# Hybrid diffusion trunk on one core: one head order in the recurrence, 128-row rate projections, and both ends of the last expert stage reordered

## The chip, the core and the metric

The kernel runs on one core of a Trainium2 chip, as one program with five engines: TensorE (PE) multiplies matrices and writes to PSUM, VectorE (DVE) and ScalarE (ACT) do elementwise work and empty PSUM, GpSimd (POOL) does elementwise work in SBUF, and SyncE (SP) issues most of the DMAs. Each engine works through its own list in order. The metric is the device time of one execution in microseconds (us).

## The reference, cut to what matters

Two layers of one trunk over 512 latent tokens and a prefix of 256 context tokens, width 1024, fp32. Each layer has a mixer and a routed mixture of experts:

```python
# mixer, one of three branches: RWKV-7, 8 heads of 64, in two directions d
a = sigmoid(a0 + al @ a_up);  decay = exp(-exp(-softplus(-(w0 + tanh(wl) @ w_up)) - 0.5))
sa = S @ kk                                  # per token, S is 64 x 64 per head
S = S * decay - outer(sa, kk * a) + outer(v, kd);   y = S @ r
# experts: 16, each takes the top 64 latent tokens (and 32 context tokens, layer 1 only)
hid = silu(xin @ w1) * (xin @ w3);  out[idx] += (hid @ w2) * gate
```

`w_up` and `a_up` are 64 x 512 for each direction. An expert has three matrices of 1024 x 1024 fp32, 12 MB. Only the latent tokens are returned, so the second layer emits no context tokens: its recurrence still runs through the context to get the state, without `y`.

## The kernel before

**Recurrence (`rwkv_phase`, L890).** Heads are worked in four pairs, the two heads of a pair in partitions 0 to 63 and 64 to 127 of the projected tiles, and the 768 tokens in 12 chunks of 64. Both directions go together (index d). So a layer has 48 chunks, each with a *window* (`window`, L636), which needs no state, and a *chain* (`chain`, L760), which carries the state from chunk to chunk. A window scales keys and queries by the decays (`kc`, `kr`), multiplies them on PE into a PSUM slot, masks the products into `sc` and `sv` (L700, L701), and inverts a triangular 64 x 64 system per head by six levels of doubling in fp16 (`nb`, `wt`, `xt`, `xx`; `xtr` is the inverse). A chain multiplies state and values with `sv` (`pz`), solves with `xtr`, corrects once, and makes the next state (`V`, L844) and `y`. Windows run up to three chunks ahead.

In this kernel the row order differs for the two heads: for head h the score rows of `kk` lie in half h and those of `k` in the other half, so each mask or scaling is done once for each head on 64 partitions:

```python
for h in range(2):
    hs, ho = slice(64 * h, 64 * h + 64), slice(64 - 64 * h, 128 - 64 * h)
    v.tensor_tensor(g.sc[hs, :, :nm, hs], ps[hs, :, h, :nm], self.scc[hs, :, :nm], ALU.mult)
    v.tensor_tensor(g.sv[ho, :, :nm, h], ps[ho, :, h, :nm], self.scc[ho, :, :nm], ALU.mult)
```

The state half of `V` and the value half change places with h in the same way; `rows` (L546) and `value_rows` (L751) lay the values out to match.

**Rates (`rates`, L554).** For each pair, segment and direction two matmuls multiply the low-rank activations `wal` (rows 0 to 63 for the decay, 64 to 127 for the learning rate) with `ups`, each on its own 64 rows: 64 matmuls in the two layers.

**Fill.** The input projections that the recurrence does not need soon (`unit`, L142: `pw` tiles with their `w_hi` and `w_lo` parts) and, in the first layer, parts of the modulation (`piece`, `pa`) are handed out behind the chain, 6.0 us of PE time a chunk in the first layer and 3.0 us in the second (`self.fills`, L1874); what is left when the last chain is done runs at the end of the phase (`self.spend(1e9)`). The order on each engine is laid down before the run by a planner, which simulates a timeline with costs of its own and takes the instruction of highest priority that its timeline has ready.

**Experts of the second layer (`experts`, L1513).** `pick` (L1583) builds the one-hot matrices `gl` of four experts, then the gates (`pga`, `gcol`) and transposed one-hots (`pgt`, `gt`); `gather` (L1641) multiplies the tokens (`xhi`, `xlo`) with `gl` into `pxi` and evicts them to `xin`, for each of eight slices of the width. `hidden` (L1690) then takes `w1` and `w3` in pairs of 1 MB (`load_e`, L1668). Twelve loads of 1 MB have buffers; the first twelve are issued ahead, and each later one waits on SP until PE has read the buffer that it overwrites. `output` (L1730) multiplies with `w2`; after each second expert `scatter` (L1783) weighs the result with gate and modulation, splits it in `yhi` and `ylo`, multiplies by `gt` (`psc`) and adds to the residual `xr` (L1803), and the end of the kernel stores `xr` from SP (L1578).

Of the kernel before, what the change touches and what calls it, by code (L numbers as in the profile page):

```python
# [19 lines left out]
P = 128  # L20
D = 1024
KT = 8
# [45 lines left out]
class Trunk:  # L68
# [168 lines left out]
    def consts(self, ctx):  # L237
# [6 lines left out]
        self.id64 = cp.tile([P, 64], F32, name="id64")  # L244
        nc.vector.tensor_tensor(self.id64, self.ident[:, 0:64], self.ident[:, 64:128], ALU.add)
# [235 lines left out]
    def lora(self, full):  # L481
# [3 lines left out]
        self.ups = rp.tile([P, 2, P], F32, name="ups")  # L485
# [12 lines left out]
    def pair(self, p, full):  # L498
# [7 lines left out]
        def load():  # L506
            for d in range(2):
                cs = slice(p * P, (p + 1) * P)
                nc.sync.dma_start(self.ups[0:64, d], self.i["rwkv_w_up"][self.l, d, :, cs])
                nc.sync.dma_start(self.ups[64:128, d], self.i["rwkv_a_up"][self.l, d, :, cs])  # L510
# [36 lines left out]
        def rows(s):  # L547

            self.need(q.u["value"])
            b0, nb = SEGB[s]  # L550
            vt = q.vt[s] = rp.tile([P, 2 * nb, HD], F32, name="vt", tag=f"vt{s}")
            self.requarter(q.v[:, b0 * P:], nb, lambda c, h: vt[64 - 64 * h:128 - 64 * h, c::2])

        def rates(s):  # L554
# [5 lines left out]
            if s == 0:  # L560
                q.f = rp.tile([P, 2, NCH], F32, name="f", tag="f", bufs=2)
                q.lm = rp.tile([P, 2, NCH], F32, name="lm", tag="lm")
            nc.gpsimd.memset(D[:, 0, :, 0:1], 0.0)
            nc.gpsimd.memset(D[:, 1, :, 64:65], 0.0)
            for d in range(2):
                w0, a0 = self.w0h[:, 4 * d + p:4 * d + p + 1], self.a0h[:, 4 * d + p:4 * d + p + 1]
                ps = self.bank()
                self.mm(ps[:, :n], self.ups[0:64, d], self.wal[0:64, a:a + n], True, True)
# [11 lines left out]
                self.mm(ps[:, :n], self.ups[64:128, d], self.wal[64:128, a:a + n], True, True)  # L580
# [14 lines left out]
            nc.scalar.activation(q.f[:, :, x], q.f[:, :, x], AF.Exp, scale=S_DEC)  # L595

# [39 lines left out]
    def window(self, q, n, emit, kb):  # L636
# [43 lines left out]
        g.sv = rp.tile([P, 2, 2, 2, 64], F32, name="sv", tag="sv", bufs=4)  # L680
        for h in range(2):
            hs, ho = slice(64 * h, 64 * h + 64), slice(64 - 64 * h, 128 - 64 * h)
            v.tensor_tensor(kc[hs, :, ho], two(q.k)[hs], t1[hs], ALU.mult)
            v.tensor_tensor(kc[hs, :, hs], kk[hs], t2[hs], ALU.mult)
            dst = g.sv[hs, :, :nm, h]
            if n:
                f = q.f[hs, :, n - 1, None, None].to_broadcast([64, 2, nm, 64])
                pl.tensor_tensor(dst, kr[hs, :, h, :nm], f, ALU.mult)
            else:
                pl.tensor_copy(dst, kr[hs, :, h, :nm])  # L690
        yield

        bank = self.slots[n % 3]
        ps = bank.rearrange("p (d h m i) -> p d h m i", d=2, h=2, m=2)
# [19 lines left out]
        nb = mat("nb")  # L714
        nc.gpsimd.tensor_tensor(
            nb, g.sc[:, :, 0], self.ident[:, None].to_broadcast([P, 2, P]), ALU.add
        )
        x = xt = None
        for l in range(6):
# [24 lines left out]
            else:  # L744
                xt = mat("xtr", F32R, "xtr", 4)
# [5 lines left out]
    def value_rows(self, q, n):  # L751

        t = self.rp.tile([P, 2, 2, HD], F32, name="V", tag="V", bufs=3)
        s, z0, z1, _ = seg_chunks(n)
        for h in range(2):
            ho = slice(64 - 64 * h, 128 - 64 * h)
            self.nc.gpsimd.tensor_copy(t[ho, :, h], self.two(q.vt[s][ho], z0, z1))
        return t

    def chain(self, q, n, V, emit):  # L760
# [4 lines left out]
        halves = [slice(0, 64), slice(64, 128)]  # L765
        if n == 0:
            V = self.value_rows(q, 0)
            for h, hs in enumerate(halves):
                nc.gpsimd.memset(V[hs, :, h], 0.0)
        last = n == NCH - 1  # L770
        out = None if last else self.value_rows(q, n + 1)
        if n and not last:
            sf = rp.tile([P, 2, HD], F32, name="sf", tag="sf")
            fc = q.f[:, :, n - 1]
            for h, hs in enumerate(halves):
# [22 lines left out]
        sa = first = None  # L798
# [39 lines left out]
        if emit:  # L838
# [1099 lines left out]
```

## Time and profile before

| | |
|---|---|
| Median of 3 runs | 3648.34 us (3643.23 to 3650.91) |
| Profiled execution, device time | 3643.64 us |
| Its span (first to last instruction) | 3641.9 us |
| PE busy | 3367.1 us (92%) |
| DVE busy | 1950.3 us (54%) |
| ACT busy | 1289.5 us (35%) |
| POOL busy | 1133.7 us (31%) |
| Weights of the experts (`we`) | 384 DMAs of 1 MB |

A busy PE is not PE at its peak: a matmul's recorded time holds its latency, and the next one starts before it ends. So PE's pace is read from start to start. An fp32 matmul has two records, an fp32r matmul one. A granted clock of 1.00 is 2.4 GHz, 0.50 is 1.2 GHz. Idle time of an engine that is not the bottleneck costs nothing; what matters is what PE or, in the second layer's expert stage, the DMA engines wait for.

### The profile page before, as it was taken

To read this page: it belongs to the slowest core of one execution; us is meant where nothing else is said; L and a number is where in the kernel's file an instruction comes from. 1 tells how busy PE (TensorE), PEld (TensorE's weight loads), DVE (VectorE), ACT (ScalarE), POOL (GpSimd) and SP (SyncE) were. 2 spreads that over 40 slices of the span, in tenths; PEclk is the share of its full clock that TensorE was granted. 3 is DMA by queue.
4 is the path that set the end of the run, shared out by engine and by line. 5 is a ranking of instruction groups with operands and counts; after the bars stand their busy time and mean duration, and the time that the engine had idled before them with its cause. 6 is when DMAs were issued, how large, how long until landed. Compare 5 with 4: busy or idle time off the path is not lost.

```text
span 3641.9 us, 56218 instructions
## 1 busy us (share of the span) xinstructions
PE 3367.1 (92%) x20863; PEld 2243.8 (62%) x20863; DVE 1950.3 (54%) x4725; ACT 1289.5 (35%) x3233; POOL 1133.7 (31%) x1729
## 2 busy tenths in 40 slices
PE   6999999999998989999999898888899989799998
PEld 3777777777987882233333477676678968543342
DVE  6687878764665461121222577878864665412122
ACT  3354555543454211111111345555553542211111
POOL 3555465543320410000000255656554303100000
PEclk9999999999998989999999899999999989899999
DMA  5323132334106336778888410111113154499998
GB/s 182 101 67 98 35 110 67 123 120 144 47 33 222 121 123 253 288 294 327 328 319 335 153 57 29 36 37 39 36 51 101 36 177 157 186 409 409 409 409 350
DMA packets 297045, 620.94 MB, mean 171 GB/s; under 512 B 19258, under 2 KB 160532, under 8 KB 296772
## 3 DMA queue, kind: packets, MB, share of 16 engines
q1 hardware_dynamic: 293028, 605.30, 46.0%
q0 software_dynamic: 1728, 6.29, 0.5%
q10 hardware_dynamic: 2016, 5.77, 0.4%
q8 instruction: 165, 2.70, 0.3%
q14 instruction: 108, 0.88, 0.1%
HBM read 584.00 MB, written 33.29 MB: 170 GB/s over the span
## 4 chain that ended last, share of the span: by engine, by line
PE 50%; DVE 9%; DMA 2%; ACT 2%; issue 2%; POOL 1%; DVEq 0%; ACTq 0%; POOLq 0%
PE ph L81 13%; PE pw L81 6%; PE py L81 6%; PE pc L81 4%; PE po L81 3%; PE slot L81 2%; PE pt L81 2%; PE psc L81 2%; PE pyc L81 2%; PE ba L81 2%; PE pz L85 2%; DMA we<-in_exp_w 2%; PE py L85 1%; PE pxi L81 1%; DVE wt L725 1%
## 5 line engine op out<-in xcount | busy, mean ns | idle before, releaser
L81 PE MATMUL ph<-we,xin 128*64 128x512 f32 x2048 | 513.3, 605 | 5.4 <-DVE hid L1721 2.8
L81 PE MATMUL pw<-hhi,w_hi 128*128 128x512 f32 (+1 forms) x1272 | 490.7, 390 | 15.0 <-ACT w_hi L132 6.7
L81 PE MATMUL pw<-hlo,w_hi 128*128 128x512 f32 (+1 forms) x1272 | 451.2, 359 | 0.0
L81 PE MATMUL pw<-hhi,w_lo 128*128 128x512 f32 (+1 forms) x1272 | 450.9, 360 | 0.3 <-POOL w_lo L134 0.3
L134 POOL TENSOR_TENSOR w_lo<-w_raw,w_hi 128x1024 fp32r<-128x1024 f32 x124 | 300.5, 2429 | 357.2 <-ACT w_hi L132 296.8
L81 PEld LDWEIGHTS ph<-we,xin 128*64 128x64 f32 x2048 | 151.0, 139 | 325.8 <-issue 315.2
L1793 POOL TENSOR_TENSOR ylo<-y,yhi 128x512 fp32r<-128x512 f32 x28 | 35.2, 1281 | 889.3 <-ACT yhi L1792 889.3
L725 DVE TENSOR_TENSOR wt<-slot,lvm 128x256 f16<-128x256 f32 x576 | 230.3, 418 | 94.0 <-PE slot L81 66.1
L81 PEld LDWEIGHTS pw<-hhi,w_hi 128*128 128x128 f32 x1272 | 243.6, 193 | 45.0 <-ACT w_hi L132 8.0
L81 PEld LDWEIGHTS pw<-hhi,w_lo 128*128 128x128 f32 x1272 | 242.1, 192 | 36.1 <-issue 2.6
L81 PEld LDWEIGHTS pw<-hlo,w_hi 128*128 128x128 f32 x1272 | 244.5, 193 | 30.6 <-issue 12.3
L132 ACT ACTIVATE w_hi<-w_raw 128x1024 fp32r<-128x1024 f32 x168 | 177.0, 1057 | 239.7 <-DMA w_raw<-in_w_in 77.8
L81 PE MATMUL py<-we,hT 128*64 128x512 f32 x1024 | 249.3, 607 | 8.3 <-DMA we<-in_exp_w 3.0
L742 ACT ACTIVATE xx<-slot 128x256 f16<-128x256 f32 x384 | 145.9, 382 | 162.8 <-PE slot L81 137.5
L1720 ACT ACTIVATE sl<-ph 64x512 f32<-64x512 f32 x64 | 37.8, 591 | 449.4 <-PE ph L81 429.7
L1803 DVE TENSOR_TENSOR xr<-xr,psc 128x512 f32<-128x512 f32 x144 | 90.4, 681 | 195.5 <-PE psc L81 195.4
L1721 DVE TENSOR_TENSOR hid<-sl,ph 64x512 f32<-64x512 f32 x64 | 44.1, 690 | 268.3 <-ACT sl L1720 267.9
L81 PEld LDWEIGHTS py<-we,hT 128*64 128x64 f32 x1024 | 70.3, 138 | 153.0 <-issue 134.4
L81 PE MATMUL pt<-w_hi,hhi 128*128 128x256 f32 x544 | 155.8, 288 | 5.4 <-ACT xk L1117 2.0
L81 PE MATMUL pt<-w_lo,hhi 128*128 128x256 f32 x544 | 155.5, 286 | 3.4 <-POOL w_lo L134 3.4
L81 PE MATMUL pt<-w_hi,hlo 128*128 128x256 f32 x544 | 154.7, 285 | 0.0
L81 PE MATMUL slot<-xt,wt 128*128 128x128 f16 x960 | 132.2, 224 | 21.6 <-DVE wt L725 21.1
(412 smaller groups left out, 7661.9 us busy)
## 6 DMA issues: line engine op xcount, KB each, us to landing
we<-in_exp_w SPq DMA_DIRECT2D x384, 1024.0 KB
w_raw<-in_w_in SPq DMA_DIRECT2D x124, 512.0 KB
ada_w<-in_ada_w SPq DMA_DIRECT2D x96, 512.0 KB
w_raw<-in_w_branch SPq DMA_DIRECT2D x24, 512.0 KB
w_raw<-in_w_out SPq DMA_DIRECT2D x20, 512.0 KB
gd<-gt SPq DMA_DIRECT2D x24, 384.0 KB
g<-gd SPq DMA_DIRECT2D x24, 384.0 KB
gd<-gt SPq DMA_DIRECT2D x24, 256.0 KB
```

The lines of the kernel that those rows point to most:

```text
L81: return self.leg(self.nc.tensor.matmul(out, lhsT, rhs, start=start, stop=stop))
L85: return self.leg(self.nc.tensor.matmul(out, lhsT, rhs, start=start, stop=True, skip_group_check=True))
L132: nc.scalar.activation(hi, raw, AF.Copy)
L134: self.lo_eng.tensor_tensor(lo, raw, hi.bitcast(F32), ALU.subtract)
L725: v.tensor_tensor(wt, ps, self.lvm[:, :, l], ALU.mult)
L742: nc.scalar.activation(x, ps2, AF.Copy)
L1720: nc.scalar.activation(sl, ph[0:64, ns], AF.Silu)
L1721: v.tensor_tensor(hid[0:64, ns], sl, ph[64:128, ns], ALU.mult)
L1793: (v if by_block else self.ylo_eng[nh]).tensor_tensor(lo, yn, hi.bitcast(F32), ALU.subtract)
L1803: v.tensor_tensor(x, x, pt, ALU.add)
```

## The change

Both heads now use one row order: `kk` rows in partitions 0 to 63, `k` and value rows in 64 to 127, and the head is an index of the free dimension. The scalings of `kc` and the masks are one instruction for both heads; the value half of `sv` is a POOL copy of `sc`; `nb` becomes two POOL instructions into a persistent, zeroed block-diagonal tile; the first solution `x1` is evicted by two ACT instructions, one for each head, and the second solution goes to PE straight from `V`, without its own copy. The rate projections get 128 rows with zeros in the unused half. In the second layer's expert stage the gather of the first group runs two slices at a time between the weight loads of its first expert, its gates come after that expert's `hidden`, and the last expert's `w2` is loaded by halves of its columns, each half scattered and stored from SP and ACT when it is done.

```diff
-        self.ups = rp.tile([P, 2, P], F32, name="ups")
...
+        self.ups = rp.tile([P, 2, 2, P], F32, name="ups")
+        nc.gpsimd.memset(self.ups, 0.0)
...
-            vt = q.vt[s] = rp.tile([P, 2 * nb, HD], F32, name="vt", tag=f"vt{s}")
-            self.requarter(q.v[:, b0 * P:], nb, lambda c, h: vt[64 - 64 * h:128 - 64 * h, c::2])
+            vt = q.vt[s] = rp.tile([P, nb, 2, HD], F32, name="vt", tag=f"vt{s}")
+            pt = self.bank().rearrange("p (b t) -> p b t", t=P)
+            for b in range(nb):
+                self.tr(pt[:, b], q.v[:, (b0 + b) * P:(b0 + b + 1) * P])
+            nc.scalar.activation(vt.rearrange("p b h x -> p b (h x)"), pt[:, :nb], AF.Copy)
...
+                q.fs = rp.tile([P, 2, 2, NCH], F32, name="f", tag="f", bufs=2)
+                q.f = q.fs[:, 0]
...
-                self.mm(ps[:, :n], self.ups[0:64, d], self.wal[0:64, a:a + n], True, True)
+                self.mm(ps[:, :n], self.ups[:, 0, d], self.wal[:, a:a + n], True, True)
...
-                self.mm(ps[:, :n], self.ups[64:128, d], self.wal[64:128, a:a + n], True, True)
+                self.mm(ps[:, :n], self.ups[:, 1, d], self.wal[:, a:a + n], True, True)
...
+            nc.gpsimd.tensor_copy(q.fs[0:64, 1, :, x], q.f[64:128, :, x])
...
-
-        kc, kr, g.sc = kb
+        kc, kr, g.sv, nb = kb
...
-            pl.tensor_tensor(kr[hs, :, h, 0], kk[hs], at(e, False)[hs], ALU.mult)
+            pl.tensor_tensor(kr[hs, :, 0, h], kk[hs], at(e, False)[hs], ALU.mult)
             if emit:
-                pl.tensor_tensor(kr[hs, :, h, 1], two(q.r)[hs], at(e, True)[hs], ALU.mult)
+                pl.tensor_tensor(kr[hs, :, 1, h], two(q.r)[hs], at(e, True)[hs], ALU.mult)
...
-        g.sv = rp.tile([P, 2, 2, 2, 64], F32, name="sv", tag="sv", bufs=4)
+        v.tensor_tensor(kc[:, :, 64:128], two(q.k), t1, ALU.mult)
+        v.tensor_tensor(kc[:, :, 0:64], kk, t2, ALU.mult)
         for h in range(2):
-            hs, ho = slice(64 * h, 64 * h + 64), slice(64 - 64 * h, 128 - 64 * h)
-            v.tensor_tensor(kc[hs, :, ho], two(q.k)[hs], t1[hs], ALU.mult)
-            v.tensor_tensor(kc[hs, :, hs], kk[hs], t2[hs], ALU.mult)
-            dst = g.sv[hs, :, :nm, h]
+            hs = slice(64 * h, 64 * h + 64)
...
+        g.sc = rp.tile([P, 2, 2, 2, 64], F32, name="sc", tag="sc", bufs=4)
...
-            self.mm(ps[:, d, :, :nm], kc[:, d], kr[:, d, :, :nm], True, True)
-        for h in range(2):
-            hs, ho = slice(64 * h, 64 * h + 64), slice(64 - 64 * h, 128 - 64 * h)
-            v.tensor_tensor(g.sc[hs, :, :nm, hs], ps[hs, :, h, :nm], self.scc[hs, :, :nm], ALU.mult)
-            v.tensor_tensor(g.sv[ho, :, :nm, h], ps[ho, :, h, :nm], self.scc[ho, :, :nm], ALU.mult)
+            self.mm(ps[:, d, :nm], kc[:, d], kr[:, d, :nm], True, True)
+        if emit:
+            fl = lambda t: t.rearrange("p d m h i -> p (d m) h i")
+            mask = self.scc.rearrange("p d m i -> p (d m) i")[:, :, None].to_broadcast([P, 4, 2, 64])
+            v.tensor_tensor(fl(g.sc), fl(ps), mask, ALU.mult)
+        else:
+            mask = self.scc[:, :, 0, None].to_broadcast([P, 2, 2, 64])
+            v.tensor_tensor(g.sc[:, :, 0], ps[:, :, 0], mask, ALU.mult)
+        pl.tensor_copy(g.sv[64:128, :, 0], g.sc[64:128, :, 0])
...
-        nb = mat("nb")
-        nc.gpsimd.tensor_tensor(
-            nb, g.sc[:, :, 0], self.ident[:, None].to_broadcast([P, 2, P]), ALU.add
-        )
+        for h in range(2):
+            hs = slice(64 * h, 64 * h + 64)
+            pl.tensor_tensor(
+                nb[hs, :, hs], g.sc[0:64, :, 0, h], self.ident[0:64, None, 0:64].to_broadcast([64, 2, 64]), ALU.add
+            )
...
-        s, z0, z1, _ = seg_chunks(n)
-        for h in range(2):
-            ho = slice(64 - 64 * h, 128 - 64 * h)
-            self.nc.gpsimd.tensor_copy(t[ho, :, h], self.two(q.vt[s][ho], z0, z1))
+        s, *z, _ = seg_chunks(n)
+        for d in range(2):
+            c = 64 * (z[d] % 2)
+            self.nc.gpsimd.tensor_copy(t[64:128, d], q.vt[s][c:c + 64, z[d] // 2])
...
-            sf = rp.tile([P, 2, HD], F32, name="sf", tag="sf")
-            fc = q.f[:, :, n - 1]
-            for h, hs in enumerate(halves):
-                nc.gpsimd.tensor_tensor(
-                    sf[hs], V[hs, :, h], fc[hs, :, None].to_broadcast([64, 2, HD]), ALU.mult
-                )
-
-
-        own = list(enumerate(halves))
-        both = lambda t, d: t[:, d, None].to_broadcast([P, 2, HD])
+            sf = rp.tile([64, 2, 2, HD], F32, name="sf", tag="sf")
+            f = q.fs[lo, :, :, n - 1].rearrange("p h d -> p d h")[:, :, :, None].to_broadcast([64, 2, 2, HD])
+            nc.gpsimd.tensor_tensor(sf, V[lo], f, ALU.mult)
...
-                    v.tensor_tensor(r[hs], zz[hs, :, h], sa[hs], ALU.subtract)
+                    v.tensor_tensor(r[hs], zz[hs, :, h], x1[lo, :, h], ALU.subtract)
...
-                sa = rp.tile([P, 2, HD], F32, name="sa", tag="sa", bufs=2)
-                nc.scalar.activation(sa, aa, AF.Copy)
+                for h, hs in own:
+                    nc.scalar.activation(x1[lo, :, h], aa[hs], AF.Copy)
                 self.mark()
                 for d in range(2):
-                    self.mma(zz[:, d], g.sc[:, d, 0], both(sa, d))
+                    self.mma(zz[:, d], g.sc[:, d, 0], x1[:, d])
...
-                nc.scalar.activation(V[hs, :, h], aa[hs], AF.Copy)
+                nc.scalar.activation(V[lo, :, h], aa[hs], AF.Copy)
             else:
-                v.tensor_copy(V[hs, :, h], aa[hs])
-        if emit:
-            sa = rp.tile([P, 2, HD], F32, name="sa", tag="sa", bufs=2)
-            nc.scalar.activation(sa, aa, AF.Copy)
+                v.tensor_copy(V[lo, :, h], aa[hs])
...
-                self.mma(yy[:, d], g.sc[:, d, 1], both(sa, d))
+                self.mma(yy[:, d], g.sc[:, d, 1], V[:, d])
...
-                    v.tensor_tensor(out[hs, :, h], pss[hs, :, h], sf[hs], ALU.add)
+                    v.tensor_tensor(out[lo, :, h], pss[hs, :, h], sf[:, :, h], ALU.add)
...
                 g = self.pick(0, full, post, aff)
-                self.gather(g, full, xhi, xlo)
+                ahead = self.gather(g, full, xhi, xlo)
+                if full:
+                    ahead = [None for _ in ahead] and None
+                else:
+                    next(ahead)
+            if not full:
+
+                hid0 = self.hidden(0, full, g, ahead)
+                self.group_gates(g, 0, full, aff)
             due, prev = [], None
...
                 due = []
-                if e:
+                if e == NE and not full:
+                    self.last_output(e - 1, *prev, g2r)
+                elif e:
                     due = self.output(e - 1, full, *prev, g2r)
                 if e % 4 == 3 and e < NE - 1:
                     with tc.high_priority(self.gather_hp):
                         nxt = new if full else self.pick(e // 4 + 1, full, post, aff)
-                        self.gather(nxt, full, xhi, xlo)
+                        if not full:
+                            self.group_gates(nxt, e // 4 + 1, full, aff)
+                        for _ in self.gather(nxt, full, xhi, xlo):
+                            pass
                 prev = hid, g
                 g = nxt or g
             with tc.high_priority(self.norm_hp):
                 for args in sorted(due, key=lambda t: t[-2]):
...
+            if k % 2:
+                yield
...
             ws = load(c)
+            if ahead and c:
+                next(ahead, None)
...
+    def last_output(self, ge, hid, g, g2r):
 
         nc, ep, psg = self.nc, self.ep, self.psg
...
         for nh in range(2):
+            ns = slice(nh * 512, nh * 512 + 512)
+            py = self.psy.tile([P, 512], F32, name="py", tag=("py", "py1")[nh])
+            for c in range(2):
+                pool = self.xwp[self.n_we % len(self.xwp)]
+                self.n_we += 1
+                w = pool.tile([P, 4, 512], F32, name="we", tag="we")
+                nc.sync.dma_start(
+                    w, self.i["exp_w2"][self.l, ge, c * 512:(c + 1) * 512, ns].rearrange("(k p) n -> p k n", p=P)
+                )
+                for kk in range(4):
+                    k = 4 * c + kk
+                    r = 64 * (k % 2)
+                    self.mm(py[r:r + 64], hT[:, k], w[:, kk], k < 2, k > 5)
+            odd = ep.tile([64, 512], F32, name="odd", tag="s", bufs=2)
+            nc.scalar.copy(odd, py[64:128])
+            v.tensor_tensor(self.y[64:128, ns], odd, py[0:64], ALU.add)
+            with self.tc.high_priority(self.norm_hp):
+                self.scatter(self.y, g.gcol[:, 1:2], g2r[0], g.gt[:, 1], 2, 4, by_block=True, halves=(nh,))
+                for b in range(2, NB):
+                    (nc.sync, nc.scalar)[b % 2].dma_start(self.out[0, (b - 2) * P:(b - 1) * P, ns], self.xs[b][:, ns])
```

## Rows read from the trace of the kernel before

**Rows 1.** Windows: stretch, length; busy us (instructions) PE, PEld, DVE, ACT, POOL; clock, DMA, GB/s.
```profile
110.00:870.00 760.00, 722.87 (x5231) 575.49 (x5229) 559.95 (x1458) 375.31 (x1098) 389.99 (x694) 0.99 0.29 95
2110.00:2750.00 640.00, 575.44 (x3958) 443.54 (x3957) 489.12 (x1308) 341.09 (x1002) 371.31 (x670) 0.97 0.13 41
2750.00:2786.00 36.00, 33.79 (x149) 26.74 (x148) 10.58 (x22) 11.77 (x21) 16.14 (x7) 1.00 0.42 137
3150.00:3160.00 10.00, 10.00 (x60) 6.26 (x62) 0.91 (x3) 3.65 (x7) 0.00 (x0) 1.00 0.29 97
3160.00:3170.00 10.00, 10.00 (x40) 2.88 (x38) 0.52 (x2) 2.48 (x3) 0.00 (x0) 1.00 0.76 265
3170.00:3620.00 450.00, 427.75 (x1958) 170.07 (x1954) 88.34 (x153) 57.98 (x107) 17.64 (x14) 0.97 1.03 409
3620.00:3630.00 10.00, 7.35 (x32) 2.03 (x32) 1.77 (x3) 1.03 (x3) 0.00 (x0) 1.00 0.37 147
```

**Rows 2.** PE's waits in 110 to 870: waiter <- releaser, us, times, longest.
```profile
PE pz L85 <- DVE V L844: 8.5, 18, 0.9
...
PE pw L81 <- DVE pv L456: 0.3, 1, 0.3
```

**Rows 3.** PE's waits in 2110 to 2770.
```profile
PE slot L81 <- DVE wt L725: 16.1, 23, 2.4
...
PE slot L108 <- DVE sv L701: 9.4, 18, 1.1
...
PE bk L81 <- DVE bv L612: 1.4, 2, 0.7
PE pz L85 <- ACT sa L827: 0.8, 2, 0.4
```

**Rows 4.** PE's timeline at a 64-row rate matmul: start, us, what.
```profile
2141.08 0.40 PE L81 MATMUL pw<-hlo,w_hi 128*128 128x512 f32 x1
2141.40 1.12 PE L81 MATMUL bk<-wal,ups 64*128 64x512 f32 x2
2142.46 0.73 PE L81 MATMUL pw<-hhi,w_lo 128*128 128x512 f32 x2
```

**Rows 5.** PE's timeline at a 128-row fp32 matmul of 512 columns.
```profile
157.32 1.02 PE L81 MATMUL bk<-bv,bones 128*128 128x512 f32 x2
158.18 0.28 PE L81 MATMUL slot<-xx,nb 128*128 128x128 f16 x2
```

**Rows 6.** Groups by form, whole span: out<-in, shape, count | busy us, mean ns | idle before.
```profile
L688 POOL TENSOR_TENSOR sv<-kr,f 64x256 f32<-64x256 f32 x152 | 100.6, 662 | 26.2 <-PE py L85 19.2 <-PE pz L85 0.2
L1803 DVE TENSOR_TENSOR xr<-xr,psc 128x512 f32<-128x512 f32 x144 | 90.4, 681 | 195.5 <-PE psc L81 195.4
L684 DVE TENSOR_TENSOR kc<-kk,t 64x128 f32<-64x128 f32 x192 | 78.6, 409 | 5.9 <-POOL t L666 5.4
L715 POOL TENSOR_TENSOR nb<-sc,ident 128x256 f16<-128x256 f32 x96 | 76.0, 792 | 50.6 <-DVE sc L700 48.8
L701 DVE TENSOR_TENSOR sv<-slot,scc 64x256 f32<-64x256 f32 x160 | 67.4, 421 | 3.3
L813 ACT ACTIVATE sa<-pz 128x128 f32<-128x128 f32 x96 | 27.3, 284 | 25.2 <-PE pz L85 24.7 <-DVE wt L725 0.3
```

**Rows 7.** Timeline of all engines, start of the second layer's expert stage.
```profile
3139.88 0.61 PE L85 MATMUL pga<-aff,gl 128*128 128x17 f32 x2 [0.78 <-DVE gl L1591]
...
3145.17 2.56 DVE L1540 TENSOR_TENSOR xlo<-xn,xhi 128x1024 fp32r<-128x1024 f32 x2
3145.28 0.55 PE L81 MATMUL pxi<-gl,xhi 128*128 128x256 f32 x1 [0.34 <-DVE gcol L1625]
...
3156.08 0.37 SPq L1675 DMA_DIRECT2D we<-in_exp_w  x1
```

**Rows 8.** Timeline at the end of the kernel.
```profile
3626.21 1.94 PE L81 MATMUL py<-we,hT 128*64 128x512 f32 x8 [0.59 <-DMA we<-in_exp_w]
...
3634.01 3.32 SPq L1578 DMA_DIRECT2D out<-xr  x4
```

More of the change, by code (lines that the diff above doesn't have):

```diff
@@ L764, in chain @@
         g = q.win.pop(n)
-        halves = [slice(0, 64), slice(64, 128)]
+        lo = slice(0, 64)
         if n == 0:
             V = self.value_rows(q, 0)
-            for h, hs in enumerate(halves):
-                nc.gpsimd.memset(V[hs, :, h], 0.0)
+            nc.gpsimd.memset(V[lo], 0.0)
         last = n == NCH - 1
@@ L797, in chain @@
         begin(zz, lambda d: g.sv[:, d, 0])
-        sa = first = None
+        x1 = self.x1[n % 2]
+        first = None
         for it in range(2):
@@ L897, in rwkv_phase @@
             self.psz = st.enter_context(tc.tile_pool(reuse_waits="tile", name="psz", bufs=1, space=PSUM))
-            kc, kr, sc = (
-                [self.rp.tile(shape, F32, name=f"{n}{a}") for a in range(m)]
-                for n, m, shape in (("kc", 2, [P, 2, P]), ("kr", 2, [P, 2, 2, 2, 64]), ("sc", 4, [P, 2, 2, P]))
+            kc, kr, sv, nb, self.x1 = (
+                [self.rp.tile(shape, dt, name=f"{n}{a}") for a in range(m)]
+                for n, m, shape, dt in (
+                    ("kc", 2, [P, 2, P], F32), ("kr", 2, [P, 2, 2, 2, 64], F32), ("sv", 4, [P, 2, 2, 2, 64], F32),
+                    ("nb", 3, [P, 2, P], F16), ("x1", 2, [P, 2, 2, HD], F32))
             )
-            for t in kr + sc:
+            for t in kr + sv + nb + self.x1:
                 nc.gpsimd.memset(t, 0.0)
@@ L949, in ahead @@
                         if n + a not in gens:
-                            gens[n + a] = self.window(q, c, full or c >= 4, (kc[c % 2], kr[c % 2], sc[(n + a) % 4]))
+                            gens[n + a] = self.window(q, c, full or c >= 4, (kc[c % 2], kr[c % 2], sv[(n + a) % 4], nb[c % 3]))
                         do(lambda: next(gens[n + a], None))
@@ L1557, in experts @@
                 if e < NE:
-                    hid = self.hidden(e, full, g)
+                    hid = hid0 if e == 0 and not full else self.hidden(e, full, g)
                 if full and e % 4 == 2 and e < NE - 2:
@@ L1575, in experts @@
                     self.scatter(*args, by_block=True)
-            if not full:
-                for b in blocks:
-                    nc.sync.dma_start(self.out[0, (b - 2) * P:(b - 1) * P, :], self.xs[b])
     def pick(self, grp, full, post, aff):
@@ L1602, in pick, with group_gates @@
                 )
+        if full:
+            self.group_gates(g, grp, full, aff)
+        return g
+    def group_gates(self, g, grp, full, aff):
+        nc, ep, psg = self.nc, self.ep, self.psg
+        v = nc.vector
+        gl, gc = g.gl, g.gc
         pt = psg.tile([P, 3, NE + 1], F32, name="pga", tag="g")
@@ L1680, in by_turns @@
     @staticmethod
-    def by_turns(latents, context, full, load):
+    def by_turns(latents, context, full, load, ahead=None):
         for c in range(4):
             ws = load(c)
+            if ahead and c:
+                next(ahead, None)
             fs = (latents, context) if full else (latents,)
@@ L1688, in by_turns, with hidden @@
                 f(c, *ws)
-    def hidden(self, ge, full, g):
+    def hidden(self, ge, full, g, ahead=None):
         nc, ep = self.nc, self.ep
@@ L1781, in output, with scatter @@
         return due
-    def scatter(self, y, gcol, g2r, gt, b0, nb, by_block=False):
+    def last_output(self, ge, hid, g, g2r):
         nc, ep, psg = self.nc, self.ep, self.psg
         v = nc.vector
-        hl = []
-        for nh in range(2):
+        hT = ep.tile([P, KT, CL], F32, name="hT", tag="hT")
+        for j in range(2):
+            pt = psg.tile([P, 4, CL], F32, name="phd", tag="g")
+            for q in range(4):
+                k = 4 * j + q
+                nc.tensor.transpose(pt[:, q], hid[:CL, k * P:(k + 1) * P], self.ident[:CL, :CL])
+            (nc.scalar.copy if j else v.tensor_copy)(hT[:, 4 * j:4 * j + 4], pt)
+        for nh in range(2):
+            ns = slice(nh * 512, nh * 512 + 512)
[18 more added lines that the diff above has]
+                    (nc.sync, nc.scalar)[b % 2].dma_start(self.out[0, (b - 2) * P:(b - 1) * P, ns], self.xs[b][:, ns])
+    def scatter(self, y, gcol, g2r, gt, b0, nb, by_block=False, halves=(0, 1)):
+        nc, ep, psg = self.nc, self.ep, self.psg
+        v = nc.vector
+        hl = {}
+        for nh in halves:
             yn = y[:, nh * 512:nh * 512 + 512]
@@ L1793, in scatter @@
             (v if by_block else self.ylo_eng[nh]).tensor_tensor(lo, yn, hi.bitcast(F32), ALU.subtract)
-            hl.append((hi, lo))
-        order = [(nh, b) for nh in range(2) for b in range(nb)]
+            hl[nh] = hi, lo
+        order = [(nh, b) for nh in halves for b in range(nb)]
         for nh, b in sorted(order, key=lambda t: t[1]) if by_block else order:
```

28 lines of the change are left out of this document (13 added, 15 removed).

## The prediction

> **What bounds the kernel now.** I read the busy shares by engine first, then the stretches, then what PE waits for in each stretch, and last the timelines at the places that the change touches. PE is the busiest engine in both recurrences, the DMA engines in the second layer's expert stage.
>
> In both recurrence stretches PE shows 95% and 90% busy, and DVE comes next with 560 of 760 us (74%) and 489 of 640 us (76%) [rows 1]. Behind the last chain runs what is left of the fill: from 2750 to 2786 PE is 94% busy with DVE at 29% [rows 1], and the code lays out the first layer's end in the same way. So each recurrence ends when PE has done its whole list, not when the chain is done, and a recurrence takes PE's own time plus PE's stalls. The stalls that end with a DVE instruction are 23.8 us in the first layer (eight rows, the longest 8.5 us for the next state, the shortest 0.3 us) [rows 2] and 53.0 us in the second (eight rows, from 16.1 us for `wt` to 1.4 us) [rows 3].
>
> The expert stage of the second layer differs. From 3170 us on the DMA engines move 409 GB/s without a gap, until about 3623.6 us (share 0.37 of the slice from 3620, against 1.03) [rows 1]. Its length is set by when the weight stream starts and what follows its last load. The thirteenth load is issued at 3156.08 us [rows 7].
>
> Layer 1's expert stage, both attentions and merges keep their work; I cost them at nothing.
>
> **The change part by part.**
>
> *Rate projections, 128 rows.* The fp32r matmul before the 64-row one keeps PE for 0.23 us (the pace of its neighbours, 0.23 to 0.24 us from start to start), so PE is free at 2141.31; the 64-row matmul starts at 2141.40, the next at 2142.46: 1.15 us [rows 4]. A 128-row fp32 matmul of 512 columns takes 158.18 - 157.32 = 0.86 us [rows 5]. The streaming time is the same; the difference of 0.29 us stands at the change of tile shape and back. With 64 such matmuls: 64 x 0.29 = 18.6 us of PE time. Those of 256 columns I take to save the same, since the loss is at the two ends. PE's list sets the end, so this is on the path; I take 17 us, and 0 to 18.6 for the range, as a saved gap can become a wait for data. The other way round, the skill speaks against padding: the Trainium skill, TensorEngine Tiling (Array Packing), Performance Considerations, says of a contraction of 64 that it should be tiled by rows, for up to twice the throughput. By that rule the decay and learning-rate matmuls, in opposite halves of the rows, would share 0.86 us and the padding would lose time. Here they stand alone between full-height matmuls, as in the row, and the trace does not agree.
>
> *DVE in the windows.* In an emitting window four `kc` instructions of about 0.409 us become two; an instruction's time follows its elements for each partition (128 here, before and after), so this saves 0.82 us. Four mask instructions of 0.421 us become one of 512 elements for each partition out of PSUM, for which I take the 0.681 us of the residual addition: 1.00 us less [rows 6]. Of 96 windows 80 emit, 16 save about 1.5 us: 80 x 1.82 + 16 x 1.5 = 170 us of DVE, 85 us in each layer, and DVE falls from about 75% to about 63% of the stretch. That is no time by itself. It buys back part of PE's stalls. The 9.4 us in which the `kc` transposes wait for the last mask [rows 3] should mostly go, since one mask of 0.68 us stands there in place of four of 1.68 us together: 8 us. Of the other 67 us (23.8 + 53.0 - 9.4) I take a quarter, 16 us: these are waits inside the chain and the doubling, where the DVE instruction itself stays and only the queue before it shortens. So 24 us. The ends are 0 (the list is laid out ahead, and PE may meet the next late instruction at once) and 77 us (all DVE stalls). What is late next is ACT, at 53% of the second layer's stretch [rows 1].
>
> *Longer hops.* `x1` is two ACT instructions in series, each near the 0.284 us of the one that it replaces [rows 6]: up to 96 x 0.28 = 27 us of chain latency. Queued behind them on ACT are the evictions of the doubling (`xx`, `xt`); PE waits for both. In emitting chunks the second `sa` copy goes, so ACT's sum stays; PE now waits for `V` there, which it needs anyway. PE's wait for `sa` is 0.8 us in the whole second stretch [rows 3], because fill lies between: I take 2 us, range -1 to 27. On POOL the value half of `sv` is one more copy of 64x256, at most 0.66 us by the multiplication of that shape, and `nb` is two halves for one of 0.79 us [rows 6]; `sf` is one instruction for two. POOL is at 51% and 58% [rows 1]. The copy lies between mask and chain, a chunk ahead of its use: 2 us, range 0 to 30. What waits in POOL's queue behind it is `nb`, and DVE's `xt` behind that. The extra zeroings at the head of each recurrence are hidden by the fill that runs there; without that cover they cost about 1 us a layer. The value layout (`rows`) loses two DVE copies a segment, and `id64` one instruction at the start, both in DVE's slack of a quarter of the stretch.
>
> *Start of the last expert stage.* Gates and one-hot transposes hold PE from 3139.88 us, and the first `pxi` comes at 3145.28 [rows 7]. With the gates behind `hidden` it can start at about 3140, limited by `xlo` of the last two blocks, which DVE does at 3145.17 after the gate columns [rows 7] and can now do right after `gl`, at about 3141 to 3143.5. Now 10.8 us lie between the first `pxi` and the thirteenth load (3156.08 - 3145.28), since PE takes several slices of `pxi` ahead of the first weights. With two slices ahead it should not take longer, so from 3140 the load comes at 3150.8 or earlier; the wait for `xlo` eats what the fewer slices save. No other DMA waits in front of it on SP. The stream of 180 loads takes 180 x 1.0486 MB / 409 GB/s = 461.5 us, against 3623.6 - 3156.1 = 467.5 us now; the slices of 29% and 76% [rows 1] show the starving. So the gain is 5.3 us of start and up to 6 us of starving; I take 7, range 0 (the planner leaves the gates in front) to 11. The gates, about 4 us of PE, move to where DMA covers them; if PE were the bound there, they would cost these 4 us.
>
> *End.* After the last load PE works 1.94 us from 3626.21, then come the evictions, weighting, splitting, eight additions and four stores, the first issued at 3634.01 [rows 8]; the span ends at 3641.9. After the change four additions remain behind the last load, 4 x 0.68 = 2.7 us less, one more step (the sum of the two halves, 0.68) is added, and the first half's additions can stand in DVE's queue before it, about 1 us. Stores are of half the size, on two queues. I take 1.5 us, range -4 to +3: four loads with rows of 2 KB have no row here, and I take them at the stream's pace.
>
> **Sum.** -17 - 24 + 2 + 2 - 7 - 1.5 = -45.5 us against the profiled execution's 3643.64, or 3598. That execution lies 4.7 us under the median of 3648.34; on the median's scale it is 3603 us, which I forecast.
>
> **The rivals.**
>
> *DVE was not what PE waited for.* The stalls are placed by the planner's order, and PE meets an equal stall elsewhere. Then only the matmul shape and both ends count: -17 + 4 - 8.5 = -21.5, or 3627 us. For it: PE's waits are spread over many releasers of a few us each [rows 2, 3]. Against: nearly all of them are DVE's.
>
> *DVE was the pace of both recurrences.* Most of 77 us goes, and the stream starves less: -18 - 65 + 2 - 11 = -92, or 3556 us. For it: 75% busy in an ordered queue. Against: PE is at 95% in layer 1, and its stalls there are 24 us.
>
> *POOL's new copy is late (slower).* The value half of `sv` now goes DVE, POOL, PE. POOL also carries the `w_lo` subtractions and works in order. If a copy is late by one such place in the queue, the first matmul of a chunk waits; at 0.8 us, about the `nb` ahead of it [rows 6], for all 96 chunks that is 77 us, less the 45.5: +31, or 3680 us. It decides when the copy's lead over its chunk falls under the queue in front of it. For it: `nb`, 0.79 us, waits 48.8 us for the masks already. Against: windows run a chunk ahead, some 13 us (640 us for 48 chunks).
>
> *It does not do what it says.* The planner lays out everything anew, and gains and new stalls cancel: 3648 us, within 7.
>
> **How the numbers follow.** Forecast (3588 to 3615) 0.42; only shape and ends (3615 to 3641) 0.24; DVE's pace (below 3588) 0.16; cancelled (within 0.2%, 3641 to 3656) 0.08; POOL late (above 3656) 0.10. 0.2%, some 7 us, is about what a measurement can tell from no change. Faster is 0.42 + 0.24 + 0.16 = 0.82, same 0.08, slower 0.10. The range leaves about 0.1 on each side: 3566 to 3645 us.
>
> **What would show it.** Right: the rate matmuls at 0.86 us from start to start; DVE's busy time 150 us or more lower; PE's waits for `V`, `wt` and the masks under 60 us together; the thirteenth load near 3150 minus what the recurrences gave; 409 GB/s from there. Wrong: PE's waits for POOL's `sv` or ACT's `x1` above 10 us; gates before the first `pxi`; a recurrence as long as now with DVE at 63%. The prediction falls if the two recurrences together give back less than 15 us.

## The result and the profile after

The changed kernel takes 3592.65 us (median of 4 runs, 3586.59 to 3597.45), the kernel before, on the same chip, 3647.66 us (3643.23 to 3650.91). The ratio is 0.9856, with a 95% interval of 0.9845 to 0.9868: 55 us or 1.4% faster, 10 us below the forecast of 3603 and inside the forecast's own range of 3588 to 3615. The profiled execution took 3593.62 us, its span 3591.8.

The busy shares of the changed kernel: busy us, share of the span, instructions.

```profile
PE 3332.6 (93%) x20863; PEld 2243.1 (62%) x20863; DVE 1799.7 (50%) x4213; ACT 1293.5 (36%) x3234; POOL 1193.1 (33%) x1861
```

DVE lost 150.6 us, POOL gained 59.4, ACT stayed. The stretches that answer to [rows 1], columns as there:

```profile
110.00:858.00 748.00, 715.35 (x5267) 579.87 (x5265) 484.75 (x1214) 377.33 (x1094) 422.51 (x765) 0.98 0.30 96
2100.00:2702.00 602.00, 552.90 (x3939) 440.00 (x3938) 417.46 (x1047) 343.17 (x1009) 400.22 (x730) 0.97 0.14 44
2702.00:2745.00 43.00, 40.30 (x200) 33.01 (x199) 11.29 (x24) 14.54 (x23) 20.42 (x11) 1.00 0.42 132
3130.00:3560.00 430.00, 412.25 (x1897) 163.50 (x1895) 84.79 (x147) 56.01 (x103) 17.64 (x14) 0.98 1.02 406
```

In the second layer's recurrence DVE is down from 76% to 69% and PE up from 90% to 92%; the last stage still moves weights at 406 GB/s. PE's waits of the changed kernel, 110 to 858 and then 2100 to 2760 (waiter <- releaser: us, times, longest), answer to [rows 2, 3]:

```profile
PE slot L81 <- DVE wt L735: 8.2, 8, 2.6
PE pz L85 <- DVE zr L809: 3.8, 5, 2.2
...
PE pz L85 <- DVE V L850: 0.8, 1, 0.8
```

```profile
PE slot L81 <- DVE wt L735: 22.3, 17, 4.7
PE pz L85 <- DVE zr L811: 4.4, 7, 1.9
PE slot L81 <- ACT xt L756: 4.2, 10, 0.8
...
PE slot L108 <- DVE sc L706: 3.3, 2, 2.5
```

The wait for the last mask fell from 9.4 us to 3.3, that for the next state nearly vanished, and the wait for `wt` grew from 16.1 to 22.3. All rows that end with DVE together fell from 23.8 to 14.5 us and from 53.0 to 36.4. No row names POOL's copy of `sv`.

The groups of the new instructions (busy us, mean ns), beside [rows 6]:

```profile
L706 DVE TENSOR_TENSOR sc<-slot,scc 128x512 f32<-128x512 f32 x80 | 55.3, 691 | 10.5 <-PE slot L81 8.2 <-PE py L85 0.5
L819 ACT ACTIVATE x<-pz 64x128 f32<-64x128 f32 x192 | 51.6, 269 | 25.6 <-PE pz L85 22.9 <-DVE wt L735 1.4
L710 POOL COPY sv<-sc 64x256 f32<-64x256 f32 x96 | 47.3, 493 | 5.8
L686 DVE TENSOR_TENSOR kc<-kk,t 128x128 f32<-128x128 f32 x96 | 45.7, 476 | 5.7 <-POOL t L672 5.6
```

The start of the last stage in the changed kernel, against [rows 7]: `pxi` follows the one-hots at once, and the thirteenth load (one of eight in this row) is issued at 3105.61.

```profile
3095.76 0.98 PE L81 MATMUL pxi<-gl,xhi 128*128 128x256 f32 x3 [0.87 <-DVE gl L1607]
...
3100.65 1.08 PE L81 MATMUL ph<-we,xin 128*64 128x512 f32 x4 [0.42 <-ACT xin L1684]
...
3105.61 17.59 SPq L1700 DMA_DIRECT2D we<-in_exp_w  x8
```

Where the 50.1 us of span went, worked out from the first and last starts of tiles: up to the router's first matmul (`lg`) of layer 1 11.5 us, the stage from there to layer 2 +0.8, layer 2's recurrence, attention and merge 33.2, from its last `lg` to the end 6.1.

### The profile page after: what moved, and what is told of

The parts are those of the page before. It is cut to its first block, busy times and chain, and to the rows that moved or that the text cites. A ratio compares the mean times of both kernels' runs of the same rounds, so it can differ in the third digit from the quotient of the medians.

```text
span 3591.8 us, 55796 instructions
## 1 busy us (share of the span) xinstructions
PE 3332.6 (93%) x20863; PEld 2243.1 (62%) x20863; DVE 1799.7 (50%) x4213; ACT 1293.5 (36%) x3234; POOL 1193.1 (33%) x1861
```

## The experiments

Differences below are those of the ratios, times 3648 us, since each ratio is taken against the kernel before on the same chip; the medians, from several chips, differ from them by up to 4 us. The table gives stages of one profiled execution each, in us: A to the first `lg`, B from there to layer 2's first rate matmul, C to the last `lg`, D to the end.

| kernel | median | ratio (95%) | A | B | C | D |
|---|---|---|---|---|---|---|
| before | 3648 | 1 | 1271.2 | 815.1 | 1033.2 | 522.3 |
| changed | 3592.65 | 0.9856 (0.9845 to 0.9868) | 1259.7 | 815.9 | 1000.0 | 516.2 |
| padding alone | 3653.56 | 1.0016 (1.0008 to 1.0025) | 1272.4 | 822.8 | 1032.0 | 522.8 |
| both ends alone | 3640.96 | 0.9987 (0.9976 to 0.9998) | 1270.5 | 815.1 | 1030.3 | 518.4 |
| head order alone | 3605.33 | 0.9885 (0.9868 to 0.9901) | 1265.5 | 811.3 | 1006.0 | 522.0 |
| changed, no padding | 3601.16 | 0.9868 (0.9851 to 0.9886) | 1260.7 | 816.6 | 1008.2 | 517.7 |
| `kc` and masks by halves | 3675.16 | 1.0078 (1.0065 to 1.0091) | 1289.0 | 820.5 | 1049.0 | 517.9 |
| masks by halves | 3618.69 | 0.9918 (0.9905 to 0.9931) | 1257.0 | 816.2 | 1025.8 | 518.6 |
| idle DVE load | 3639.56 | 0.9974 (0.9965 to 0.9984) | 1265.4 | 822.7 | 1025.9 | 518.6 |
| zeroed early | 3587.93 | 0.9838 (0.9826 to 0.9851) | 1253.1 | 815.6 | 1000.5 | 517.0 |
| `x1` evicted twice | 3617.74 | 0.9921 (0.9906 to 0.9936) | 1262.8 | 814.7 | 1022.1 | 515.1 |
| `sv` copied twice | 3601.00 | 0.9880 (0.9865 to 0.9895) | 1249.4 | 816.2 | 1018.7 | 515.2 |
| gates in front | 3592.85 | 0.9854 (0.9836 to 0.9871) | 1255.5 | 816.4 | 999.8 | 520.9 |
| `kk` half of `kc` on POOL | 3583.64 | 0.9828 (0.9816 to 0.9841) | 1250.1 | 815.8 | 999.9 | 516.5 |

**The three parts.** First each part on the kernel before. Padding alone:

```diff
-self.ups = rp.tile([P, 2, P], F32, name="ups")
+self.ups = rp.tile([P, 2, 2, P], F32, name="ups")
+nc.gpsimd.memset(self.ups, 0.0)
...
-self.mm(ps[:, :n], self.ups[0:64, d], self.wal[0:64, a:a + n], True, True)
+self.mm(ps[:, :n], self.ups[:, 0, d], self.wal[:, a:a + n], True, True)
...
```

> The kernel before with the rate projections padded to 128 rows and nothing else. Theory A (the 0.29 us at each change of tile shape is PE time on the path): 64 x 0.29 = 18.6 us of pace goes, and the time falls by 15 to 19 us, ratio near 0.9955; the rate matmuls then take 0.86 us from start to start. Rival B (a saved gap is only traded for a wait): the pace of the rate matmuls falls as in A, but the time falls by less than 8 us, ratio above 0.998.

It came out 6 us slower, so theory A failed and rival B's condition held. The matmuls themselves did what was predicted: from start to start, layer 2's rate matmuls take 19.7 us in place of 27.0. But PE's gaps in that stretch (2118 to 2778, before 2110 to 2770) grew from 66.8 to 70.7 us, and stage C gained 1.2 us of these 7.3. The longest waits there have hardly moved against [rows 3]:

```profile
PE slot L81 <- DVE wt L726: 16.3, 23, 2.4
...
PE slot L108 <- DVE sv L702: 9.7, 18, 1.1
```

At the head of layer 1, PE waits 3.7 us for the loads of `ups`, which stand behind the new zeroing. Stage B, which the edit doesn't touch, is 7.7 us longer; what makes it so stays open. In the stages that it does touch its effects cancel (A +1.2, C -1.2), so the 6 us are no price of the padding: it is worth nothing there.

Both ends alone (the expert stage's part of the diff):

```diff
-                self.gather(g, full, xhi, xlo)
+                ahead = self.gather(g, full, xhi, xlo)
...
+                hid0 = self.hidden(0, full, g, ahead)
+                self.group_gates(g, 0, full, aff)
...
+                if e == NE and not full:
+                    self.last_output(e - 1, *prev, g2r)
```

> The kernel before with only the second layer's expert stage changed at both ends. Theory A (the weight stream sets that stage, and it starts as much earlier as the gates move back): time falls by 5 to 8 us, of which 5 to 6 at the start and 0 to 2 at the end, ratio 0.9978 to 0.9986. Rival B (PE, not the stream, sets the stage, and pays for the gates later): under 2 us, ratio above 0.9995.

5 us faster (6 by the medians), 3.9 of them in stage D by the profile: at the lower end of what was expected. The head order alone (recurrence as in the change, 64-row rates, old expert stage):

```diff
-            v.tensor_tensor(kc[hs, :, ho], two(q.k)[hs], t1[hs], ALU.mult)
-            v.tensor_tensor(kc[hs, :, hs], kk[hs], t2[hs], ALU.mult)
...
+        v.tensor_tensor(kc[:, :, 64:128], two(q.k), t1, ALU.mult)
+        v.tensor_tensor(kc[:, :, 0:64], kk, t2, ALU.mult)
...
```

> The kernel before with only the one head order (64-row rates and the old expert stage stay). Theory A (DVE's load goes down by some 150 us and PE's stalls with it): the two recurrences together give 20 to 30 us, more of it in the second layer, ratio 0.992 to 0.9945. Rival B (the gain of the whole change beyond padding and ends comes from a luckier layout of the lists): alone the head order gives less than 10 us or loses, ratio above 0.997.

42 us faster by the ratio, more than the 20 to 30 that were expected and about twice what the sum had for it; 27 of them are in stage C and 6 in stage A. Last the changed kernel with 64-row rates:

```diff
-self.mm(ps[:, :n], self.ups[:, 0, d], self.wal[:, a:a + n], True, True)
+self.mm(ps[:, :n], self.ups[0:64, d], self.wal[0:64, a:a + n], True, True)
...
```

> The changed kernel with 64-row rate projections again. Theory A (parts add up): 15 to 19 us slower than the changed kernel, so some 37 us faster than before, ratio near 0.990. Rival B (padding and head order cover the same stalls): within 8 us of the changed kernel, ratio below 0.988.

4 us slower than the change (8.5 by the medians), with intervals that overlap: far under theory A, and as its rival B said. Stage C is 8.2 us longer, where the padding alone gained 1.2. By that stage the padding pays only once DVE is relieved; the totals are too close to show it. The parts add up: 42 + 5 + 4 = 51 against (1 - 0.9856) x 3648 = 53.

**What in the head order gained.** In the changed kernel, `kc` and masks by halves again, then the masks alone:

```diff
-v.tensor_tensor(fl(g.sc), fl(ps), mask, ALU.mult)
...
+for h in range(2):
+    for rs in (slice(0, 64), slice(64, 128)):
+        v.tensor_tensor(g.sc[rs, :, :nm, h], ps[rs, :, :nm, h], self.scc[rs, :, :nm], ALU.mult)
```

> The changed kernel with the scalings of kc and the masks done by halves again (four and four DVE instructions in an emitting window in place of two and one), the new row layout kept. DVE gets back some 150 us. Theory A, DVE's load is what the head order relieved: 20 to 40 us over the changed kernel, 3613 to 3633. Theory B, the gain came from elsewhere in the head order (the copy of the second solution on ACT that is gone, the layout of the values, the order as laid down): within 8 us of the changed kernel, 3585 to 3601.

> Only the masks by halves again: four of about 0.42 us in place of one of 0.69 in 80 windows, DVE +80 us. Theory A in proportion to the load: 10 to 22 us over the changed kernel. Theory C, the length of the mask step counts, since the products wait for its last instruction, and not the load: as much as with both split. Theory B: within 4 us.

And DVE instructions whose result nothing reads:

```diff
+for j in range(3 + emit):
+    v.tensor_tensor(t2, t2, t1, ALU.mult)
```

> The changed kernel with four more DVE instructions in an emitting window (three in another), each about 0.45 us, that multiply t2 in place behind its last reader; nobody reads the result. DVE +160 us and no step of window or chain is longer by itself. Theory A (load): 20 to 40 us over the changed kernel, as with both split. Theory C (length of the steps): within 8 us, while both split is slow. Theory B: within 8 us.

23 us for the masks (DVE +79.7), 43 us for the idle load (DVE +123.3), 81 us for both splits (DVE +154.0): all three above theory A's ranges, the first two just so. Theory B is out, since the splits take away more than the head order gained. For a microsecond of DVE's busy time the masks cost 0.28 us and the idle load 0.35. Of the idle load's 43 us, 6.8 stand in stage B, which the edit doesn't touch; without them it costs 0.29.

This is not the price of DVE's load by itself. `t1` and `t2` have one buffer each, and the idle instructions multiply in them, so ACT and POOL, which make the next window's `t1` and `t2`, wait for the idle instructions. Who waits for these (us, times), and then who waits for the two `kc` instructions of the changed kernel:

```profile
  POOL t L672: 91.4, 57
  ACT t L666: 81.6, 70
```

```profile
  ACT t L666: 32.8, 37
  POOL t L672: 9.2, 18
```

The masks leave `t1` and `t2` alone, but lengthen the step in front of the products, so theory C isn't excluded for them. What DVE's load costs without such a longer hold or step, no run shows. The idle load and the masks cost the second layer and hardly the first: stage C grows by 26 us with each, stage A by 5.7 with the idle load and by -2.7 with the masks. Both splits cost more than their load: 58 us for the `kc` part alone, where 74 us of load would give 22 to 26. The rest may be the longer way to the products, which wait for the last `kc`, or the hold, since ACT and POOL wait 73.7 and 48.5 us for `kc` there. That stays open.

How the idle load acts is seen in the second recurrence, in the changed kernel and then with the load (windows, columns as in [rows 1]), and in PE's waits with the load:

```profile
2126.00:2703.00 577.00, 527.90 (x3822) 420.02 (x3821) 406.06 (x1023) 333.41 (x990) 380.14 (x699) 0.97 0.14 43
```

```profile
2139.00:2745.00 606.00, 544.20 (x3826) 429.25 (x3825) 464.77 (x1196) 335.34 (x991) 387.58 (x701) 0.95 0.13 41
```

```profile
PE slot L81 <- DVE wt L737: 25.4, 25, 4.3
PE pz L85 <- DVE zr L813: 5.5, 8, 2.4
...
PE pz L85 <- DVE zr L811: 4.0, 7, 2.3
```

29 us more for the same matmuls. In these windows gaps between matmuls (length less PE) grew by 13 us, and the matmuls themselves, from start to start, by 16: the mean granted clock fell from 0.97 to 0.95, and 0.02 of 606 us is 12. In this recurrence a wait is paid about twice, once as a gap and once as slower work. In the first layer's it is not (same two kernels):

```profile
122.00:840.00 718.00, 685.44 (x5095) 557.03 (x5093) 469.61 (x1181) 368.15 (x1075) 407.79 (x739) 0.98 0.30 96
```

```profile
121.00:847.00 726.00, 683.78 (x5097) 552.33 (x5096) 528.62 (x1366) 370.41 (x1077) 413.55 (x741) 0.99 0.30 95
```

There the gaps grew by 10 us, but the clock did not fall and the matmuls took 2 us less.

**What the head order paid.** Twice the evictions of `x1`, and twice the POOL copy of `sv`:

```diff
 for h, hs in own:
     nc.scalar.activation(x1[lo, :, h], aa[hs], AF.Copy)
+    nc.scalar.activation(x1[lo, :, h], aa[hs], AF.Copy)
```

```diff
 pl.tensor_copy(g.sv[64:128, :, 0], g.sc[64:128, :, 0])
+pl.tensor_copy(g.sv[64:128, :, 0], g.sc[64:128, :, 0])
```

> The changed kernel with each ACT eviction of the first solution x1 done twice, the same values written again: four instructions of about 0.28 us in series behind one solve where the change has two and the kernel before had one. The run with both split, at DVE's load of before, was some 28 us slower than before with padding and ends; if that cost is the longer hop of x1, doubling the excess and more gives 15 to 54 us over the changed kernel. If the hop lies beside the fill, as predicted (2 us): within 6 us.

> The changed kernel with the POOL copy of the value half of sv done twice: POOL +50 to 60 us, and every later POOL instruction of a window (nb among them) half a microsecond later. If POOL's queue is what the head order paid with: 10 to 30 us over the changed kernel. If POOL has room, as predicted (2 us): within 6 us.

The first costs 24 us (0.9921 against 0.9856), inside what was expected if the hop counts, with 192 more instructions of 0.269 us, 51.6 us of chain: about half of it is on the path. Its waits in the second recurrence (2100 to 2740):

```profile
PE slot L81 <- DVE wt L735: 20.1, 23, 4.7
PE pz L85 <- ACT x L820: 6.7, 10, 1.6
PE slot L81 <- ACT xt L756: 6.4, 12, 1.2
```

The wait for `x1` is up from 0.2 to 6.7 us, that for `xt`, which stands behind it on ACT, from 4.2 to 6.4. The change added one such instruction a chunk, 96, so an estimate by the same half is 12 us. The second kernel costs 9 us for 42 us of POOL, between the two expectations, its interval (0.9865 to 0.9895) just overlapping the change's. No wait for the copy appears; PE waits 0.7 us for POOL's `nb`, and its wait for `wt` on DVE, 22.3 us in the changed kernel, is longer (2100 to 2730):

```profile
PE slot L81 <- DVE wt L736: 28.6, 25, 4.5
```

Its stage C is 18.7 us longer, but its first stage is 10 us shorter though it only adds work. The planner lays everything out anew, and a stage can move by that much, so no single number here is better than some 8 us unless the stage that was edited shows it too, and POOL's 9 us are hardly more than that.

**The zeroing, the gates, and a further step.** In the changed kernel POOL zeroes `ups` at 69.3 us, and PE stands idle for it (timeline of PE, then windows):

```profile
71.94 1.19 PE L81 MATMUL bk<-wal,ups 128*128 128x256 f32 x2 [4.67 <-DMA ups<-in_rwkv_w_up]
...
74.21 0.63 PE L81 MATMUL pw<-hhi,w_hi 128*128 128x512 f32 x1
74.64 0.63 PE L81 MATMUL pw<-hlo,w_hi 128*128 128x512 f32 x1
```

```profile
60.00:70.00 10.00, 7.28 (x41) 6.08 (x39) 4.17 (x7) 2.75 (x5) 8.25 (x21) 1.00 0.01 2
70.00:80.00 10.00, 8.06 (x24) 6.43 (x25) 1.42 (x3) 0.47 (x1) 2.46 (x3) 0.66 0.22 66
```

```diff
-nc.gpsimd.memset(self.ups, 0.0)
+with self.tc.high_priority(self.piece_hp):
+    nc.vector.memset(self.ups, 0.0)
```

> The changed kernel with the zeroing of ups put early on DVE in place of POOL's queue, where it ran at 69.3 us and held the loads of ups and, behind them, PE for 4.7 us. If that wait and the half clock behind it are lost time: 4 to 6 us under the changed kernel, about 3587. Rival: the first layer's recurrence gives the 5 us back elsewhere: within 2 us.

7 us faster (4.7 by the medians) with intervals that overlap, 6.6 of them in stage A, where the edit is: as expected. The wait for the loads is 2.2 us, and the clock holds:

```profile
70.00:80.00 10.00, 9.79 (x55) 8.45 (x55) 4.07 (x7) 2.18 (x5) 2.44 (x3) 1.00 0.22 62
```

So padding without its zeroing in POOL's queue is worth 4 + 7 = 11 us here (0.9838 against 0.9868, intervals that just touch). The gates of the first expert group in front again:

```diff
 else:
+    self.group_gates(g, 0, full, aff)
     next(ahead)
...
-    self.group_gates(g, 0, full, aff)
```

> The changed kernel with the gates and transposed one-hots of the first expert group in front of its gather again. By the traces the head of the last expert stage gives 5.6 us: 4 to 7 us over the changed kernel, with the first pxi some 4 to 5 us later against the last lg. Rival, the order of gates and gather costs nothing and the slices of two made the gain: within 2 us.

The stage did as expected, 4.7 us longer (D), with the first `pxi` 5.5 us later against the last `lg`:

```profile
3091.93 0.61 PE L85 MATMUL pga<-aff,gl 128*128 128x17 f32 x2 [0.78 <-DVE gl L1607]
...
3097.34 0.55 PE L81 MATMUL pxi<-gl,xhi 128*128 128x256 f32 x1 [0.34 <-DVE gcol L1649]
```

The total did not move: stage A, which the edit doesn't touch, is 4.2 us shorter. By the stage the head of the expert stage is worth about 5 us; by the total it isn't told from nothing.

Last, DVE relieved further: the changed kernel zeroed early, with `kc`'s `kk` half on POOL.

```diff
-v.tensor_tensor(kc[:, :, 0:64], kk, t2, ALU.mult)
+pl.tensor_tensor(kc[:, :, 0:64], kk, t2, ALU.mult)
```

> The changed kernel with ups zeroed early on DVE, and the kk half of kc made on POOL, where t2 is made: DVE -46 us, POOL some +60 us. By the load theory, at 0.32 to 0.39 us of time for one of DVE's load (26 for 79 us, 47 for 123): 15 to 18 us under the kernel zeroed early (3588), 3570 to 3573. Rival, POOL, 67% busy in the second layer's recurrence, has no room for it: 3588 to 3610. Rival, below today's load DVE is no longer what decides: 3584 to 3590.

4 us faster than zeroed early, with intervals that overlap: the fastest kernel of this study by its median, but far from the 15 to 18 us that were expected, and about a third of what the idle load's price would give. Its busy shares:

```profile
PE 3330.2 (93%) x20863; PEld 2240.8 (63%) x20863; DVE 1766.0 (49%) x4119; ACT 1292.2 (36%) x3234; POOL 1232.1 (34%) x1955
```

DVE -35 us and POOL +40 against zeroed early. At 0.35 for DVE and 9 / 42 = 0.2 for POOL that is -12 + 8 = -4 us, which fits; but both prices are loose, so that POOL's price took the rest isn't shown, nor is it excluded that DVE no longer decides below today's load.

## Why the prediction was right, and where its steps were not

The total and the sign held, and so did what each part does to its instructions. The times of the terms did not, and that the sum came within 10 us is in part luck: DVE's term was some 39 us too small, and against it stand 13 us too much for the padding with its zeroing, 17 too little for the cost of the hops and 3.5 too much for the ends.

- **What bounds the kernel: half right.** The last stage is DMA's, as said. That a recurrence takes PE's list plus its stalls is true as a sum, but in the kernel before a saving on the list came back as a wait (padding alone).
- **Padding, -17: mis-sized by its cover.** The size was right: from start to start the rate matmuls took 8.2 and 8.9 us less in the two layers, 0.27 us for each of the 64. It was worth 11 us with DVE relieved, 4 with the zeroing, nothing before. "The extra zeroings at the head of each recurrence are hidden by the fill" failed in layer 1: the loads of `ups` stand behind the zeroing, and PE behind the loads.
- **DVE relief, -24: about half of what it was, or less.** The instructions were nearly right (150.6 us less against 170; one mask is 0.691 us against 0.681). PE's recorded waits for DVE fell by 9.3 + 16.6 = 26 us, close to the predicted number; but 150 us at the idle load's price would be 44 to 53 us, the two splits cost 81, and the head order's own 42 with the hops' 21 below make 63. The step that failed, "Of the other 67 us I take a quarter", took PE's waits for the whole price: in the second recurrence the slower clock behind them counted again, 16 us beside 13 with the idle load. The earlier release of `t1` and `t2` may be part of the gain as well: ACT and POOL waited 52.9 and 49.8 us for `kc` before and 32.8 and 9.2 after.
- **Longer hops, +2 and +2: too low.** `x1` is about 12 us by the doubling, POOL's copy about 9 (with an interval that overlaps the change's), both inside the stated ranges. "Fill lies between" was wrong for `x1`: PE's wait in the kernel before showed how the list had been laid out around one hop, not what a second hop would cost.
- **Ends, -8.5: 5 to 6 measured.** The thirteenth load came at 3105.6, where "near 3150 minus what the recurrences gave" puts it at 3106. The new end was not run apart from the new start.
- **The rivals.** "DVE was not what PE waited for" falls with the two splits, "does not do what it says" with the parts. "DVE was the pace" was the better account of the term, though not of the total. POOL's copy is no wait of PE; that POOL's work has a price is likely from stage C (18.7 us) and not shown by the total.

With measured sizes: padding -11, zeroing +7, DVE -63, hops +21, ends -5: -51, where the prediction had -17, 0, -24, +4 and -8.5. The -63 is what the head order's -42 leaves for DVE, not a measurement of its own.

## What to carry to other kernels

Where several engines share a chain, price an engine's load by adding idle instructions to it: PE's recorded waits for that engine showed only about half of what the head order gained here. Let the idle instructions use a tile of their own; in a tile that others wait for they price the hold as well. Read the price by stage, since one layer paid it here and the other hardly did. A saving on the busiest engine pays only as far as what it waits for moves too, so it may be worth nothing alone and most of its size beside another edit. A new zeroing in front of a load is a link of a chain: follow it to whoever waits for the load.

## What the runs showed of the hardware

**A stall can be paid twice.** In 60 to 70 us of the changed kernel the granted clock is 1.00 (2.4 GHz). Behind the stall of 4.67 us `pw` matmuls of 512 columns start every 0.43 us in place of 0.23, and the clock of the slice is 0.66, a mean of the levels 1.2 and 2.4 GHz. With the padding alone, where the stall is 3.7 us, the same slice has 0.83; zeroed early, with a stall of 2.2 us, it stays at 1.00.

**DVE held behind POOL.** `xt`, `kc` and `wt` on DVE in the changed kernel (duration min/median/max, ns):

```profile
L739 DVE TENSOR_TENSOR xt<-nb,lvm x96: 273/293/2459, 118.2 to 2672.8; 128x256 f16<-128x256 f16 x96
...
L686 DVE TENSOR_TENSOR kc<-kk,t x96: 276/284/2439, 104.0 to 2649.2; 128x128 f32<-128x128 f32 x96
...
L735 DVE TENSOR_TENSOR wt<-slot,lvm x576: 391/424/427, 121.4 to 2688.3; 128x256 f16<-128x256 f32 x192
```

The longest `xt` in the timeline, beside POOL:

```profile
2649.86 2.36 POOL L134 TENSOR_TENSOR w_lo<-w_raw,w_hi 128x1024 fp32r<-128x1024 f32 x1
...
2649.91 2.46 DVE L739 TENSOR_TENSOR xt<-nb,lvm 128x256 f16<-128x256 f16 x1
```

Both its inputs lie in SBUF; it starts 0.05 us behind POOL's `w_lo` and ends 0.15 us after it, eight times its median. `wt`, with one input from PSUM, never takes over 0.427 us. The Trainium skill, SBUF — State Buffer, Who interferes with whom, says that a DVE instruction with two SBUF inputs contends with a GpSimd instruction that reads SBUF, and that issue order decides which of the two blocks; this trace agrees. So the 0.41 us that the prediction took for a `kc` is a mean over a median of 0.28 us and a tail up to 2.47 us; that the whole tail is such holding isn't shown. It is no source of the gain: over `kc` and `xt` the time above 285 ns sums to 59 us before and after. No run here took POOL's work away.
